# Values of two attention groups, and outputs and statistics of the second, laid out in DRAM with longer rows, and row halves and sums in a third ring buffer

## The chip, the cores and the metric

The kernel runs on one core of a Trainium2 chip. The metric is the time of one execution on the device in microseconds (us); smaller is better. The core has five engines that run their own instruction streams and wait for each other through semaphores: PE (matrix products), DVE (vectors), ACT (scalar functions and copies), POOL (general) and SP, which here issues nearly all transfers between DRAM and the on-chip memory, in one fixed order.

## The reference, cut to what matters

One decoder block over 1024 tokens of 1024 numbers, in float32:

```python
h = rms_norm(x, g_pre_mix)
z = h @ w_in                                  # q, k, v | conv input (2 x 1024) | two gates
# 3 groups of 8 heads of 64; group g attends with dilation 1, 4, 16 and windows 128, 512, 2048:
s = q @ k.T / 8 + bias;  lse = logsumexp(s);  o_g = exp(s - lse) @ v      # per group and head
o = sum_g softmax_g(lse)[g] * o_g             # the three groups merged per head
y_attn = o @ w_attn_out
y_conv = silu(layer_norm(depthwise_conv31(u * sigmoid(gate)))) @ w_conv_out + b
x = x + rms_norm((sigmoid(z_ga) * y_attn + sigmoid(z_gc) * y_conv) @ w_mix_out)
x = x + rms_norm(swiglu_ffn(rms_norm(x)))     # hidden width 2816
```

## The kernel before, in words

Every float32 operand of a matrix product is split into a high part (a cast on ACT) and a low part (a subtraction on DVE or POOL), and a product is three matmuls: high x high, high x low, low x high. The work runs in stages, by the time of the profile: start and first norm (0 to 44 us), gates and conv inputs by plain products (L305, L307, L309; to 109), pairs of weight tiles by a 2x2 Winograd scheme (L321 to L323; q, k and conv inputs, to 555), the value projections with the attention woven in (to about 870), conv and attention outputs and the mix (to about 1134), the FFN's input pairs by the same scheme (to 1510) and its output (L1843).

A Winograd pair takes two loads of 128x1024, `row1` and `row2`, and makes from their quarters the sums s12 and s34 (L215/L216 and L222/L223, on POOL in the q/k stretch, on DVE elsewhere). Each is split by `both` (ACT's cast L195, then the subtraction L196); L231/L232 split the last quarter. The products are copied out of PSUM by ACT (L335, L340, L345) before PE goes on. While pairs run, POOL also adds up channels (L706) and DVE works on the convolution (L684). In the gates, the normalised input is split on DVE at L584 after ACT's cast, and weights by ACT L188 and DVE L189; ACT L1179 and DVE L1180 split other operands.

`v()` makes the values of four heads at a time (L940, L942, L944) and interleaves them with attention steps (`beat`, `tick`). Its weights w_v are loaded and split some ticks after the call by `timed`; ACT copies the products into a tile x (L950, L952) and SP stores it to the DRAM tensor dv (L927). The attention takes 12 head pairs (three groups, four pairs) of eight steps: scores (L1038), bias and minimum on DVE (L1041, the bias tile comes by L477 from the DRAM tensor rep), exponential on ACT (L1051), transposes (L1074, copies L1079/L1080), product with the values (L1095/L1097, values loaded by L903 to L908 and split by L916/L917), reduction on DVE into the output tile O (L1102). For the first two groups O goes to the DRAM tensor datt and the statistics to dst (L1060, L1064); `merge` reads both back (L887, L893) in the order of the third group. dact holds the activated conv channels (L1237).

Tiles come from pools of equal buffers that are used in turn: `slot` (tag b, 43 buffers of 128x1024), `ring` (tag d, 2 buffers of the same size; O of groups 0 and 1 and, in the mix, the new x) and `half` (tag c, 11 of 128x512). A new tile waits until the last reader of the tile that held its buffer is done. The order of instructions on each engine is the order in which the code is written, with `later` and `timed` putting steps some ticks on. SP works its list in order; each transfer also waits for the one that was issued eight before it.

Of the kernel before, what the change touches and what calls it, by code (L numbers as in the profile page):

```python
# [43 lines left out]
PLAIN = 2  # L44

LAST = 5
NSLOT = 43

NRING = 2
NHALF = 11  # L50


# [10 lines left out]
class Build:  # L63
# [108 lines left out]
    def load_ahead(self, i):  # L172
        while self.sent < min(len(self.jobs), i + 1):
            j = self.sent
            src, n, _ = self.jobs[j]
            self.raw[j] = self.slot()
            self.nc.sync.dma_start(self.raw[j][:, :n], src)
            self.sent += 1

# [19 lines left out]
    def quarters(self, i, c):  # L199


        nc = self.nc
        if c == 0:
            self.hl[i] = {}
        o = self.hl[i]
        r1, r2 = self.raw[i - 1], self.raw[i]
        a11, a12, a21, a22 = r1[:, :H], r1[:, H:], r2[:, :H], r2[:, H:]
        add = self.wsplit.tensor_tensor
        l, r = slice(0, H), slice(H, 2 * H)
        if c == 0:  # L210
            h, w = self.both(r1)
            o["A11"], o["A12"] = (h[:, l], w[:, l]), (h[:, r], w[:, r])
        elif c == 1:
            self.s12 = self.slot()
            add(self.s12[:, l], a21, a22, op=OP.add)  # L215
            add(self.s12[:, r], self.s12[:, l], a11, op=OP.add)  # L216
        elif c == 2:
            h, w = self.both(self.s12)
            o["S1"], o["S2"] = (h[:, l], w[:, l]), (h[:, r], w[:, r])
        elif c == 3:  # L220
            self.s34 = self.slot()
            add(self.s34[:, l], a11, a21, op=OP.add)  # L222
            add(self.s34[:, r], self.s12[:, r], a12, op=OP.add)  # L223
            self.s12 = None
        elif c == 4:
            h, w = self.both(self.s34)
            o["S3"], o["S4"] = (h[:, l], w[:, l]), (h[:, r], w[:, r])
            self.s34 = None
        else:
            x = self.slot(F32R)  # L230
            nc.scalar.copy(x[:, l], a22)  # L231
            add(x[:, r], a22, f(x[:, l]), op=OP.subtract)  # L232
            o["A22"] = (x[:, l], x[:, r])
            del self.raw[i], self.raw[i - 1], self.hl[i]
# [662 lines left out]
    def values(self, g, hp):  # L897

        x = self.slot()
        d = x.rearrange("p (u e) -> p u e", u=8)  # L900
        src = self.d_v[g, hp]
        if g == 0:
            self.nc.sync.dma_start(d, src.rearrange("(u p) e -> p u e", p=128))  # L903
        elif g == 1:
            for b in range(2):
                self.nc.sync.dma_start(d[:, b::2, :], src.rearrange("(b p c) e -> b p c e", b=2, c=4)[b])
        else:
            self.nc.sync.dma_start(d, src.rearrange("(p u) e -> p u e", u=8))  # L908
        return x

    def value_parts(self, x, i):

# [7 lines left out]
    def v(self, g, hg, now, then):  # L920

        nc = self.nc
        W = self.timed(now, then, 6, 15)

        def out(i, x):
            for e in range(2):
                nc.sync.dma_start(self.d_v[g, 2 * hg + e].rearrange("(t p) c -> p t c", p=128)[:, i - 2:i + 2],  # L927
                                  x.rearrange("p (t e c) -> p t e c", t=4, e=2)[:, :, e])
            self.vn += i == 6

        for i in range(0, 8, 2):
            ps = self.bank()
            for e in range(2):
                t = slice((i + e) * 128, (i + e + 1) * 128)
                o = ps[:, e * 256:(e + 1) * 256]
                for kt in range(KT):
                    hi, lo = W[kt // 4]
                    s = slice((kt % 4) * 256, (kt % 4 + 1) * 256)
                    a, b = self.hH[kt][:, t], self.hL[kt][:, t]
                    nc.tensor.matmul(o, a, hi[:, s], start=kt == 0, stop=False)  # L940
                    self.beat()
                    nc.tensor.matmul(o, a, lo[:, s], start=False, stop=False)  # L942
                    self.beat()
                    nc.tensor.matmul(o, b, hi[:, s], start=False, stop=kt == KT - 1)  # L944
                    self.beat()
                    if kt % 2:
                        self.tick()
            if i % 4 == 0:
                x = self.slot()
                nc.scalar.copy(x[:, :H], ps)  # L950
            else:
                nc.scalar.copy(x[:, H:], ps)  # L952
                self.later(2, lambda i=i, x=x: out(i, x))
                x = None

# [67 lines left out]
    def att_s(self, a, p, V, u):  # L1023
# [16 lines left out]
        for hh in range(2):  # L1040
            nc.vector.tensor_tensor_reduce(sp[:, hh * 256:hh * 256 + n], ps[:, hh * 256:hh * 256 + n],  # L1041
                                           bt[:, hh * 256 + 256 - n:(hh + 1) * 256], 1.0, 3e38, OP.add, OP.min,
                                           st[:, g, u, hh:hh + 1])
        a.update(g=g, hp=hp, u=u, blocks=blocks, sp=sp, V=V, p=p, n=n)

    def att_e(self, a):
        nc = self.nc
        sp, n, g, u = a["sp"], a["n"], a["g"], a["u"]
        st = a["p"][4]
        for hh in range(2):  # L1050
            nc.scalar.activation(sp[:, hh * 256:hh * 256 + n], sp[:, hh * 256:hh * 256 + n], AF.Exp, scale=-1.0,  # L1051
                                 bias=st[:, g, u, hh:hh + 1], accum_out=st[:, g, u, 2 + hh:3 + hh])
        if u == 7 and g < 2:
            self.tokens_out(g, self.d_st[g, a["hp"]], st[:, g])

    def tokens_out(self, g, dst, src):

        if g == 0:
            d = dst.rearrange("(u p) e -> p u e", p=128)
            self.nc.sync.dma_start(d, src)  # L1060
        else:
            d = dst.rearrange("(b p c) e -> b p c e", b=2, c=4)
            for b in range(2):
                self.nc.sync.dma_start(d[b], src[:, b::2, :])  # L1064

    def att_t(self, a):

# [15 lines left out]
    def att_p(self, a):  # L1083
# [5 lines left out]
        for hh in range(2):  # L1089
            o = hh * 128  # L1090
            for i, kb in enumerate(a["blocks"]):
                c = (kb % 4) * 256 + hh * 128
                v = a["V"][kb // 4]
                s = slice((hh * nb + i) * 128, (hh * nb + i + 1) * 128)
# [4 lines left out]
            yield 0  # L1099
        if u == 0:  # L1100
            self.O = self.ring() if g < 2 else self.slot()
        nc.vector.tensor_reduce(self.O[:, u * 128:(u + 1) * 128].rearrange("p (h c) -> p h c", h=2),  # L1102
                                ps[:, :256].rearrange("p (h e c) -> p h c e", h=2, e=2), AX.X, OP.add)
        if u == 7:
            if g < 2:
# [226 lines left out]
def build(ctx, tc, aps):  # L1332
# [38 lines left out]
    B.d_q = {n: [B.dram.tile([128, H], F32, name=f"dq{n}_{p}") for p in range(FT // 2)]  # L1371
             for n in ("A11", "A12", "A22", "S1", "S2", "S3", "S4")}
    B.d_att = {(g, hp): B.dram.tile([T, 128], F32, name=f"datt{g}{hp}") for g in range(2) for hp in range(4)}
    B.d_v = {(g, hp): B.dram.tile([T, 128], F32, name=f"dv{g}{hp}") for g in range(3) for hp in range(4)}
    B.d_ot = [B.dram.tile([128, 1024], F32, name=f"dot{p}") for p in range(2)]
    B.d_st = {(g, hp): B.dram.tile([T, 4], F32, name=f"dst{g}{hp}") for g in range(2) for hp in range(4)}

# [581 lines left out]
```

## Time and profile before

| what | us |
| --- | --- |
| median of 3 runs | 1733.87 (1732.55 to 1734.95) |
| the profiled execution | 1728.74 |
| its span (first to last instruction) | 1726.9 |
| PE busy in the span | 1703.5 |
| DVE, ACT, POOL busy | 1237.1, 793.7, 462.5 |
| values and attention, 555 to 870: PE busy | 308.61 of 315.00 |

Times in the rows of the profile are from the start of the span. In a row of the timeline stand start, duration, engine, line, operation, out<-in with their shapes, and in brackets the idle time of the engine just before and what ended it. In a row of waits stand the waiting engine and line, what it waited for, the total in us, the number of waits and the longest. Names give the pool: b is a slot, d a ring, c a half, p PSUM. In a row on DMA issues stand the number of issues, the size of one and the median time from issue to landing.

### The profile page before, as it was taken

To read this page: it belongs to the slowest core of one execution; us is meant where nothing else is said; L and a number is where in the kernel's file an instruction comes from. 1 tells how busy PE (TensorE), PEld (TensorE's weight loads), DVE (VectorE), ACT (ScalarE), POOL (GpSimd) and SP (SyncE) were. 2 spreads that over 40 slices of the span, in tenths; PEclk is the share of its full clock that TensorE was granted. 3 is DMA by queue.
4 is the path that set the end of the run, shared out by engine and by line. 5 is a ranking of instruction groups with operands and counts; after the bars stand their busy time and mean duration, and the time that the engine had idled before them with its cause. 6 is when DMAs were issued, how large, how long until landed. Compare 5 with 4: busy or idle time off the path is not lost.

```text
span 1726.9 us, 24514 instructions
## 1 busy us (share of the span) xinstructions
PE 1703.5 (99%) x8698; PEld 1448.2 (84%) x8698; DVE 1237.1 (72%) x2217; ACT 793.7 (46%) x1552; POOL 462.5 (27%) x337
## 2 busy tenths in 40 slices
PE   8999999999999999999999999999999999999998
PEld 7778888887888999999788888888888888888886
DVE  6879988789998576687664855676556555677686
ACT  6344343434444486667622346643333333454453
POOL 0017777787786043443300120000000000000000
PEclk9999999999999999999999999999999999999999
DMA  4342344345667898988945732223322322395334
GB/s 164 125 160 86 110 160 133 135 159 184 206 164 194 246 257 200 245 227 213 310 145 187 275 107 93 83 73 112 126 92 92 112 108 92 137 363 159 107 126 153
DMA packets 185398, 277.03 MB, mean 160 GB/s; under 512 B 55185, under 2 KB 106892, under 8 KB 185276
## 3 DMA queue, kind: packets, MB, share of 16 engines
q1 hardware_dynamic: 184876, 274.97, 50.2%
q8 instruction: 68, 1.11, 0.3%
q14 instruction: 54, 0.44, 0.1%
q10 hardware_dynamic: 288, 0.27, 0.0%
q0 software_dynamic: 112, 0.24, 0.0%
HBM read 184.81 MB, written 95.33 MB: 162 GB/s over the span
## 4 chain that ended last, share of the span: by engine, by line
PE 86%; POOL 5%; DVE 3%; DMA 3%; ACT 2%; issue 2%; SPq 0%; DVEq 0%; POOLq 0%; ACTq 0%
PE p L321 13%; PE p L322 13%; PE p L323 13%; PE p L1843 12%; PE p L1572 5%; PE p L305 5%; PE p L307 5%; PE p L309 5%; PE p L942 2%; PE p L940 2%; PE p L944 2%; POOL b L196 2%; PE p L554 2%; PE p L1038 2%; PE p L1074 2%
## 5 line engine op out<-in xcount | busy, mean ns | idle before, releaser
L321 PE MATMUL p<-b,b 128*128 128x512 f32 x1204 | 469.4, 390 | 3.7 <-ACT c L335 2.4
L323 PE MATMUL p<-b,b 128*128 128x512 f32 x1204 | 468.8, 389 | 0.2 <-POOL b L196 0.2
L322 PE MATMUL p<-b,b 128*128 128x512 f32 x1204 | 468.5, 389 | 0.0
L321 PEld LDWEIGHTS p<-b,b 128*128 128x128 f32 x1204 | 226.0, 188 | 53.7 <-ACT c L335 3.2
L323 PEld LDWEIGHTS p<-b,b 128*128 128x128 f32 x1204 | 226.0, 188 | 48.5 <-POOL b L196 1.3
L322 PEld LDWEIGHTS p<-b,b 128*128 128x128 f32 x1204 | 226.0, 188 | 46.4
L195 ACT CAST b<-b 128x1024 fp32r<-128x1024 f32 x131 | 137.8, 1052 | 178.4 <-DVE b L216 50.9
L1843 PE MATMUL p<-b,b 128*128 128x512 f32 x924 | 209.6, 389 | 0.0
L1843 PEld LDWEIGHTS p<-b,b 128*128 128x128 f32 x924 | 173.4, 188 | 36.0
L196 POOL TENSOR_TENSOR b<-b,b 128x1024 fp32r<-128x1024 f32 x66 | 158.8, 2406 | 116.3 <-ACT b L195 108.1
L196 DVE TENSOR_TENSOR b<-b,b 128x1024 fp32r<-128x1024 f32 x65 | 79.5, 1222 | 128.9 <-ACT b L195 128.9
L684 DVE SCALAR_TENSOR_TENSOR p<-b,par,p 128x511 f32<-128x511 f32 (+14 forms) x232 | 163.4, 738 | 0.0
L305 PE MATMUL p<-b,b 128*128 128x512 f32 x368 | 147.6, 401 | 0.0
L309 PE MATMUL p<-b,b 128*128 128x512 f32 x368 | 146.2, 397 | 0.0
L307 PE MATMUL p<-b,b 128*128 128x512 f32 x368 | 146.1, 397 | 0.0
L940 PE MATMUL p<-b,b 128*128 128x256 f32 x384 | 115.3, 300 | 0.0
L942 PE MATMUL p<-b,b 128*128 128x256 f32 x384 | 114.6, 298 | 0.0
L944 PE MATMUL p<-b,b 128*128 128x256 f32 x384 | 114.5, 298 | 0.0
L1180 DVE TENSOR_TENSOR b<-c,b 128x512 fp32r<-128x512 f32 x101 | 69.9, 693 | 46.9 <-ACT b L1179 46.6
L1179 ACT CAST b<-c 128x512 fp32r<-128x512 f32 x101 | 62.4, 618 | 63.8 <-DMA c<-dqA 19.8
L1179 ACT CAST b<-b 128x512 fp32r<-128x512 f32 x117 | 72.4, 619 | 40.6 <-DVE b L387 13.7
L1180 DVE TENSOR_TENSOR b<-b,b 128x512 fp32r<-128x512 f32 x117 | 80.3, 690 | 14.8 <-ACT b L1179 13.1
(226 smaller groups left out, 2994.1 us busy)
## 6 DMA issues: line engine op xcount, KB each, us to landing
b<-w_in SPq DMA_DIRECT2D x53, 512.0 KB, 5.7
b<-w_fi SPq DMA_DIRECT2D x44, 512.0 KB, 4.9
dk<-c SPq DMA_DIRECT2D x48, 256.0 KB, 5.7
dq<-c SPq DMA_DIRECT2D x48, 256.0 KB, 4.3
b<-dq SPq DMA_DIRECT2D x48, 256.0 KB, 8.9
b<-dk SPq DMA_DIRECT2D x48, 256.0 KB, 7.3
dqS<-c SPq DMA_DIRECT2D x44, 256.0 KB, 2.1
b<-w_fo SPq DMA_DIRECT2D x44, 256.0 KB, 5.3
```

Of the source, the lines that this page charges most:

```text
L196: self.wsplit.tensor_tensor(lo, x, f(hi), op=OP.subtract)
L305: nc.tensor.matmul(ps, hi[:, s], a, start=kt == 0, stop=False)
L307: nc.tensor.matmul(ps, hi[:, s], b, start=False, stop=False)
L309: nc.tensor.matmul(ps, lo[:, s], a, start=False, stop=kt == nk - 1)
L321: nc.tensor.matmul(ps, hi[:, s], a, start=first and kt == 0, stop=False, skip_group_check=True)
L322: nc.tensor.matmul(ps, hi[:, s], b, start=False, stop=False, skip_group_check=True)
L323: nc.tensor.matmul(ps, lo[:, s], a, start=False, stop=kt == 3, skip_group_check=True)
L684: nc.vector.scalar_tensor_tensor(A[i][:, j:], src[i][:, :H - j], w[i], A[i][:, j:], op0=OP.mult, op1=OP.add)
L940: nc.tensor.matmul(o, a, hi[:, s], start=kt == 0, stop=False)
L942: nc.tensor.matmul(o, a, lo[:, s], start=False, stop=False)
L1180: nc.vector.tensor_tensor(s[:, 512:512 + n], src, f(s[:, :n]), op=OP.subtract)
L1843: nc.tensor.matmul(acc[t], x, y, start=first and e == 0, stop=last and e == 2, skip_group_check=True)
```

## The change

The slots go from 43 to 42 and the rings from 2 to 3. The row1 loads, s12 and the values' output tile x move from slots to rings. The DRAM tensor dv of group 0 becomes 128 x 1024 (partition by token block and channel), so that it is stored by 128x512 and loaded by 128x1024. For group 1, `place` puts the eight blocks of 128 positions in another order on chip, so that values are loaded, and outputs and statistics stored, by one transfer with 2 KB rows (64 B for the statistics), where two with 512 B (16 B) were. In `v()` the loads of the next w_v are released 4 ticks after the call instead of 6, and their splits 16 instead of 15.

```diff
-NSLOT = 43
-NRING = 2
+NSLOT = 42
+NRING = 3
...
     def load_ahead(self, i):
...
-            self.raw[j] = self.slot()
+            self.raw[j] = self.ring() if kind == "row1" else self.slot()
...
         elif c == 1:
-            self.s12 = self.slot()
+            self.s12 = self.ring()
...
     def values(self, g, hp):
         x = self.slot()
-        d = x.rearrange("p (u e) -> p u e", u=8)
         src = self.d_v[g, hp]
         if g == 0:
-            self.nc.sync.dma_start(d, src.rearrange("(u p) e -> p u e", p=128))
+            self.nc.sync.dma_start(x, src)
         elif g == 1:
-            for b in range(2):
-                self.nc.sync.dma_start(d[:, b::2, :], src.rearrange("(b p c) e -> b p c e", b=2, c=4)[b])
+            self.nc.sync.dma_start(x.rearrange("p (b f) -> p b f", b=2),
+                                   src.rearrange("(b p c) e -> p b (c e)", b=2, c=4))
...
+    def place(g, u):
+        return u % 2 * 4 + u // 2 if g == 1 else u
...
     def v(self, g, hg, now, then):
-        W = self.timed(now, then, 6, 15)
+        W = self.timed(now, then, 4, 16)
         def out(i, x):
             for e in range(2):
+                if g == 0:
+                    nc.sync.dma_start(self.d_v[g, 2 * hg + e][:, (i - 2) * 128:(i + 2) * 128], x[:, e * H:(e + 1) * H])
+                    continue
...
             if i % 4 == 0:
-                x = self.slot()
-                nc.scalar.copy(x[:, :H], ps)
+                x = self.ring()
+            if g == 0:
+                nc.scalar.copy(x.rearrange("p (e t c) -> p t e c", e=2, t=4)[:, i % 4:i % 4 + 2],
+                               ps.rearrange("p (t e c) -> p t e c", t=2, e=2))
             else:
-                nc.scalar.copy(x[:, H:], ps)
+                nc.scalar.copy(x[:, (i % 4) * 256:(i % 4) * 256 + H], ps)
...
     def tokens_out(self, g, dst, src):
...
-            d = dst.rearrange("(b p c) e -> b p c e", b=2, c=4)
-            for b in range(2):
-                self.nc.sync.dma_start(d[b], src[:, b::2, :])
+            self.nc.sync.dma_start(dst.rearrange("(b p c) e -> p b (c e)", b=2, c=4),
+                                   src.rearrange("p (b c) e -> p b (c e)", b=2))
...
# statistics st[:, g, u], value blocks kb and output columns u are taken at place(g, u)
...
-    B.d_v = {(g, hp): B.dram.tile([T, 128], F32, name=f"dv{g}{hp}") for g in range(3) for hp in range(4)}
+    B.d_v = {(g, hp): B.dram.tile([T, 128] if g else [128, T], F32, name=f"dv{g}{hp}") for g in range(3) for hp in range(4)}
```

On PE, DVE, ACT and POOL the order of instructions stays the same; what moves is SP's list and the waits. Line numbers behind the edits grow by up to 13 (L927 becomes L935 or L933, L1064 becomes L1074, L1180 becomes L1193, L1237 becomes L1250).

SP at the third call of `v()`, around 612 us, before (dact are stores of the conv's activations, dv of values, dq loads for the attention):

```order
L1237 DMA dact_83<-b_5358 128x1024
L1237 DMA dact_84<-b_5374 128x1024
L177 DMA b_5389<-w_v 128x1024
L177 DMA b_5391<-w_v 128x1024
L1237 DMA dact_85<-b_5394 128x1024
```

and with the change:

```order
L1250 DMA dact_83<-b_5358 128x1024
L177 DMA b_5373<-w_v 128x1024
L177 DMA b_5375<-w_v 128x1024
L1250 DMA dact_84<-b_5378 128x1024
L1250 DMA dact_85<-b_5394 128x1024
```

The two loads of w_v stand one store earlier.

SP at the end of a head pair of the second group, around 823 us, before (rep is the source of the bias tile, dst takes the statistics):

```order
L873 DMA b_8643<-dk_117 64x1024 x2
L1064 DMA datt_220<-d_8376 512x1x128 x2
L908 DMA b_8672<-dv_232 128x1024
L477 DMA c_8682<-rep_980 128x2x256
L866 DMA b_8821<-dq_120 64x1024
L867 DMA b_8822<-dq_120 64x1024
L1064 DMA dst_243<-stat_8146 512x1x4 x2
```

and with the change:

```order
L873 DMA b_8634<-dk_117 64x1024 x2
L1074 DMA datt_220<-d_8368 128x2x512
L907 DMA b_8662<-dv_232 128x1024
L477 DMA c_8672<-rep_980 128x2x256
L866 DMA b_8811<-dq_120 64x1024
L867 DMA b_8812<-dq_120 64x1024
L1074 DMA dst_243<-stat_8139 128x2x16
```

One transfer stands in the place of two, ahead of the value load and the bias tile.

DVE with what each instruction waits for, at the split of the normalised input (first three rows, around 65 us) and at the first pair's s12 (last three, around 111 us), before:

```order
L584 TENSOR_TENSOR b_729<-b_251,b_695 128x1024 [waits DVE_49]
L579 SCALAR_TENSOR_TENSOR b_253<-b_253,gains,b_570 128x1024
L584 TENSOR_TENSOR b_750<-b_252,b_717 128x1024 [waits PE_49,Activation_49]
...
L1180 TENSOR_TENSOR b_1049<-b_253,b_1049 128x512 [waits Activation_49]
L215 TENSOR_TENSOR b_1058<-b_939 128x512 [waits DMAHW2_49,PE_49]
L216 TENSOR_TENSOR b_1058<-b_1058,b_937 128x512 [waits DVE_49]
```

and with the change:

```order
L584 TENSOR_TENSOR b_729<-b_251,b_695 128x1024 [waits PE_49]
L579 SCALAR_TENSOR_TENSOR b_253<-b_253,gains,b_570 128x1024
L584 TENSOR_TENSOR b_750<-b_252,b_717 128x1024 [waits PE_49,Activation_49]
...
L1193 TENSOR_TENSOR b_1049<-b_253,b_1049 128x512 [waits Activation_49]
L215 TENSOR_TENSOR d_1058<-b_939 128x512 [waits DMAHW2_49]
L216 TENSOR_TENSOR d_1058<-d_1058,d_937 128x512 [waits DVE_49]
```

The first L584 waits for PE now, and s12 (L215, a ring d) waits for its load alone.

More of the change, by code (lines that the diff above doesn't have):

```diff
@@ L174, in load_ahead @@
             j = self.sent
-            src, n, _ = self.jobs[j]
-            self.raw[j] = self.slot()
+            src, n, kind = self.jobs[j]
+            self.raw[j] = self.ring() if kind == "row1" else self.slot()
             self.nc.sync.dma_start(self.raw[j][:, :n], src)
@@ L899, in values @@
         x = self.slot()
-        d = x.rearrange("p (u e) -> p u e", u=8)
         src = self.d_v[g, hp]
         if g == 0:
-            self.nc.sync.dma_start(d, src.rearrange("(u p) e -> p u e", p=128))
+            self.nc.sync.dma_start(x, src)
         elif g == 1:
-            for b in range(2):
-                self.nc.sync.dma_start(d[:, b::2, :], src.rearrange("(b p c) e -> b p c e", b=2, c=4)[b])
+            self.nc.sync.dma_start(x.rearrange("p (b f) -> p b f", b=2),
+                                   src.rearrange("(b p c) e -> p b (c e)", b=2, c=4))
         else:
-            self.nc.sync.dma_start(d, src.rearrange("(p u) e -> p u e", u=8))
+            self.nc.sync.dma_start(x, src.rearrange("(p u) e -> p (u e)", u=8))
         return x
+    @staticmethod
+    def place(g, u):
+        return u % 2 * 4 + u // 2 if g == 1 else u
     def value_parts(self, x, i):
@@ L948, in v @@
             if i % 4 == 0:
-                x = self.slot()
-                nc.scalar.copy(x[:, :H], ps)
-            else:
-                nc.scalar.copy(x[:, H:], ps)
+                x = self.ring()
+            if g == 0:
+                nc.scalar.copy(x.rearrange("p (e t c) -> p t e c", e=2, t=4)[:, i % 4:i % 4 + 2],
+                               ps.rearrange("p (t e c) -> p t e c", t=2, e=2))
+            else:
+                nc.scalar.copy(x[:, (i % 4) * 256:(i % 4) * 256 + H], ps)
+            if i % 4:
                 self.later(2, lambda i=i, x=x: out(i, x))
@@ L1042, in att_s @@
                                            bt[:, hh * 256 + 256 - n:(hh + 1) * 256], 1.0, 3e38, OP.add, OP.min,
-                                           st[:, g, u, hh:hh + 1])
+                                           st[:, g, self.place(g, u), hh:hh + 1])
         a.update(g=g, hp=hp, u=u, blocks=blocks, sp=sp, V=V, p=p, n=n)
@@ L1048, in att_e @@
         sp, n, g, u = a["sp"], a["n"], a["g"], a["u"]
-        st = a["p"][4]
+        st = a["p"][4][:, g, self.place(g, u)]
         for hh in range(2):
             nc.scalar.activation(sp[:, hh * 256:hh * 256 + n], sp[:, hh * 256:hh * 256 + n], AF.Exp, scale=-1.0,
-                                 bias=st[:, g, u, hh:hh + 1], accum_out=st[:, g, u, 2 + hh:3 + hh])
+                                 bias=st[:, hh:hh + 1], accum_out=st[:, 2 + hh:3 + hh])
         if u == 7 and g < 2:
-            self.tokens_out(g, self.d_st[g, a["hp"]], st[:, g])
+            self.tokens_out(g, self.d_st[g, a["hp"]], a["p"][4][:, g])
     def tokens_out(self, g, dst, src):
@@ L1091, in att_p @@
             for i, kb in enumerate(a["blocks"]):
+                kb = self.place(g, kb)
                 c = (kb % 4) * 256 + hh * 128
@@ L1101, in att_p @@
             self.O = self.ring() if g < 2 else self.slot()
-        nc.vector.tensor_reduce(self.O[:, u * 128:(u + 1) * 128].rearrange("p (h c) -> p h c", h=2),
+        w = self.place(g, u)
+        nc.vector.tensor_reduce(self.O[:, w * 128:(w + 1) * 128].rearrange("p (h c) -> p h c", h=2),
                                 ps[:, :256].rearrange("p (h e c) -> p h c e", h=2, e=2), AX.X, OP.add)
```

## The prediction

> **What bounds the kernel now.** I read the page first (span, busy time, slices), then the waits of PE, then for each wait the timeline and the chain of waits around it.
>
> ```profile
> span 1726.9 us, 24514 instructions
> PE 1703.5 (99%) x8698; PEld 1448.2 (84%) x8698; DVE 1237.1 (72%) x2217; ACT 793.7 (46%) x1552; POOL 462.5 (27%) x337
> ...
> PE p L554 <- ACT b L530: 6.0, 1, 6.0
> PE p L1097 <- DVE c L1080: 3.7, 5, 1.2
> PE p L321 <- ACT c L335: 2.4, 2, 2.0
> PE p L1038 <- DVE stat L1041: 1.3, 1, 1.3
> PE p L321 <- ACT c L340: 1.0, 3, 0.6
> PE p L1095 <- DVE d L1102: 0.5, 1, 0.5
> PE p L1095 <- DVE b L1102: 0.3, 1, 0.3
> PE p L1038 <- DMA b<-dk: 0.2, 1, 0.2
> PE p L323 <- POOL b L196: 0.2, 1, 0.2
> ...
> 555.00:870.00 315.00, 308.61 (x2514) 299.43 (x2514) 219.06 (x666) 205.54 (x598) 104.15 (x121) 1.00 0.88 239
> ```
>
> PE is busy 1703.5 of 1726.9 us and the change takes no matmul away. So what can be won is idle time of PE: these nine rows of waits (total us, times, longest us) add up to 15.6, of which 6.0 at L554 come before any edited line. Of the 9.6 that remain, 6.0 lie in the attention stage (the rows of L1097, L1038 and L1095; the window row's 315.00 − 308.61 = 6.4 agrees), where the clock is full (1.00) and the DMA engines are 0.88 busy, and 3.6 lie around the Winograd pairs. Every term below is one of these rows.
>
> **The change part by part.**
>
> *Rows of DRAM.* The first group's values are stored in 2 KB instead of 512 B rows and loaded in 4 KB rows; the second group's values are loaded, and its outputs stored, in 2 KB rows. Each is four tensors of 1024x128 numbers, 512 KB: 4 x 4 x 512 KB = 8.4 MB in longer rows, no byte fewer. Two windows of that stage, in which DMA is busy throughout, bound the price:
>
> ```profile
> DMA packets 1593, 3.11 MB, mean 311 GB/s; under 512 B 105, under 2 KB 942, under 8 KB 1592
> ...
> DMA packets 3002, 2.96 MB, mean 269 GB/s; under 512 B 1151, under 2 KB 2431, under 8 KB 3000
> ```
>
> The first window (612 to 622 us) carries mostly longer rows, the second (823 to 834) mostly short ones. 8.4 MB at 269 GB/s are 31.2 us, at 311 GB/s 27.0: 4.2 us of DMA time in 315. That is spread over the stage and reaches PE only where a load is the late thing, so I take 0 for the row length itself, with ends 0 and −4.2. The Trainium skill ("DMA: Bandwidth & Descriptors", Specifications) puts the smallest transfer at line rate at 512 B; by that rule only the 16 B statistics gain, and the sum would have 0 here too. The trace half agrees: the window with the short rows moved 269 GB/s, a little less.
>
> *Place of the value weights in SP's queue.* The loads of w_v are released two ticks earlier, so they stand ahead of a store of dact that waits for ACT:
>
> ```profile
> 611.25 1.59 SPq L1237 DMA_DIRECT2D dact<-b  x2
> 612.93 2.43 SPq L177 DMA_DIRECT2D b<-w_v  x2
> 620.03 0.62 ACT L188 CAST b<-b 128x512 fp32r<-128x512 f32 x1 [1.56 <-DMA b<-w_v]
> ```
>
> The load is issued at 612.93 and ends ACT's idle at 620.03; DVE's L189 follows, DVE's L1041 stands behind it, and PE's L1038 waits 1.3 for that. Ahead of the two stores' end the load can go about 1.59/2 = 0.8 us earlier, and 512 KB less lies before it: at 311 GB/s 1.7 us at most. So it lands 0.8 to 2.5 earlier: −0.8 to −1.3 (the whole stall). I take −1.3, since 0.8 already counts without any help from the data and most of the 1.7 is needed by nobody else. The stores that are pushed back feed loads long after. At one place further on, w_v is moved past loads of the attention instead, a bias tile among them. 1 MB at 311 GB/s is 3.4 us; a bias tile that came 3.56 us late (next fence) cost PE 1.2. So that is one end, +1.2; I add 0, since an earlier w_v is mostly through before the tile is issued.
>
> *One store for two.* The second group's output goes out as one DMA, and its statistics too. Behind them in SP's queue stand a value load and then the bias tile (rep):
>
> ```profile
> 823.45 2.16 SPq L1064 DMA_DIRECT2D datt<-d  x2
> 826.37 0.39 SPq L477 DMA_DIRECT2D c<-rep  x1
> 832.33 0.29 DVE L1041 CUSTOM_DVE_ANT_0 c<-p,c 128x128 f32<-128x128 f32 x1 [3.56 <-DMA c<-rep]
> ...
> 833.50 0.30 PE L1097 MATMUL p<-b,c 128*128 128x64 f32 x1 [1.20 <-DVE c L1080]
> 856.25 0.30 PE L1097 MATMUL p<-b,c 128*128 128x64 f32 x1 [1.21 <-DVE c L1080]
> ...
> DVE c L1041 <- DMA c<-rep: 4.9, 2, 3.6
> ```
>
> DVE stood 3.56 us for this tile and 4.9 − 3.6 = 1.3 for the next one (the other of the two); behind both, L1080 came late and PE's L1097 stood 1.2 each time, 2.4 in all. The pair of stores takes 2.16, so with one alone the tile is issued at least 2.16/2 = 1.1 earlier. That covers nearly all of PE's 1.2, if the tile's landing follows its issue. It need not, because each DMA in this queue also waits for the one eight issues before it, and at 0.88 busy the engines set the landing. Ends 0 and −2.4; I take the half, −1.2.
>
> *Weights' first rows and the sums s12 in the ring.* Slots are reused in turn, so s12 waited for whatever held its slot. At the first pair that was a weight in use by PE; the chain of waits runs through it, and then DVE and ACT are late for PE:
>
> ```profile
> 111.66 0.69 DVE L215 TENSOR_TENSOR b<-b 128x512 f32<-128x512 f32 x1 [3.06 <-PE p L307]
> 117.14 0.62 ACT L1179 CAST b<-b 128x512 fp32r<-128x512 f32 x1 [1.25 <-DVE b L196]
> 119.27 0.50 PE L321 MATMUL p<-b,b 128*128 128x512 f32 x1 [1.99 <-ACT c L335]
> ```
>
> In the ring L215 needs only its load (the order printed with the change shows the PE wait gone), so it starts up to 3.06 earlier and everything behind it on DVE with it. ACT's L1179 gains what it waited (1.25) and what its DVE source gains; PE's 1.99 is smaller than 3.06, so I take −2.0, with 0 as the other end (if the copies ahead of L335 are late for another reason).
>
> Later the same slot reuse made ACT's cast of s12 wait for POOL's channel sum (L706), on which it does not depend:
>
> ```profile
> 324.51 1.05 ACT L195 CAST b<-b 128x1024 fp32r<-128x1024 f32 x1 [4.90 <-POOL b L706]
> 325.64 2.40 POOL L196 TENSOR_TENSOR b<-b,b 128x1024 fp32r<-128x1024 f32 x1 [1.16 <-ACT b L195]
> ...
> ACT b L195 <- POOL b L706: 22.4, 5, 4.9
> 412.00 0.50 PE L321 MATMUL p<-b,b 128*128 128x512 f32 x1 [0.56 <-ACT c L340]
> ```
>
> Freed, the cast runs beside L706, and POOL's L196 follows L706 without the 1.16. In this stretch POOL is the late engine: PE's L321 waits for L340, which stands on ACT behind casts that wait for POOL, as the last row shows in the worst case; the waits of PE asked for 340 to 460 us alone give the whole 1.0 of that row and the 0.2 of L323 <- L196. Five such pairs save about 1.16 each; I take the 1.2 of PE's two rows, ends 0 and −1.6 (each stall also delays the start of the next matmul a little).
>
> The second L335 wait (2.4 − 2.0 = 0.4), at the FFN's first pair, sits behind the same kind of chain: −0.2, half of it. Ends 0 and −0.4.
>
> *One slot fewer.* The relief through the rings starts with the first pair; before that, in the gates, 42 slots do the work of 43, and the split of the normalised input waits for PE to give one up:
>
> ```profile
> 66.49 1.23 DVE L584 TENSOR_TENSOR b<-b,b 128x1024 fp32r<-128x1024 f32 x1 [0.90 <-PE p L309]
> 72.82 0.39 PE L307 MATMUL p<-b,b 128*128 128x512 f32 x1
> 74.14 0.69 DVE L189 TENSOR_TENSOR b<-b,b 128x512 fp32r<-128x512 f32 x1 [5.83 <-ACT b L188]
> 77.72 0.69 DVE L189 TENSOR_TENSOR b<-b,b 128x512 fp32r<-128x512 f32 x1 [0.56 <-ACT b L188]
> 81.25 0.39 PE L309 MATMUL p<-b,b 128*128 128x512 f32 x1
> ```
>
> In the order the first L584 gains a PE wait, and the second gets its slot from a later product, that of the L307 at 72.82. It then starts at 73.2 instead of 66.49, 6.7 us later, of which 5.83 are the idle that stood before L189: 0.9 remain, and up to 2.4 where ACT's copies between the two are pushed as well. The second L189 ends at 78.41, and PE first reads its half near 81.25: 2.8 us of margin. I take +0.2; ends 0 and +2.4.
>
> The values' outputs now share the three rings with the attention's. Taken in turn, the closest reuse is the copy below, which gets the ring that the store above it empties:
>
> ```profile
> 647.68 0.36 SPq L1060 DMA_DIRECT2D datt<-d  x1
> 662.41 0.58 ACT L950 COPY b<-p 128x512 f32<-128x512 f32 x1 [0.90 <-PE p L944]
> ...
> dv<-b SPq DMA_DIRECT2D x24, 256.0 KB, 6.3
> datt<-d SPq DMA_DIRECT2D x8, 256.0 KB, 8.5
> ```
>
> 14.7 us lie between issue and reuse, and such stores land 6.3 and 8.5 us after issue: 0. The eight ACT copies in another shape move the same elements: 0.
>
> **The sum.** −1.3 −1.2 −2.0 −1.2 −0.2 +0.2 = −5.7 us. The profiled execution took 1728.74 us; the median of the runs is 1733.87, 5 us more, and the sum is carried to it unchanged: 1728.2.
>
> **The rivals.**
> *Long rows help all of the attention stage.* The Trainium skill ("Perfetto Trace Analysis", DMA Optimizations) says that small DMAs, under 2 KB, carry significant overhead per transfer, and that merging them helps most where DMA is the bound. As a mechanism of this kernel: loads land earlier everywhere at 0.88 busy, and all of the stage's 6.4 us go instead of 2.5. Then the sum is −9.6, 1724.3 us. Against it: only 0.2 of PE's waits name a DMA directly, and 269 against 311 GB/s is a small step.
> *The late thing is only exchanged.* DVE is still late by its own bunching (L1102 0.5 + 0.3, and two of the five L1097), the bias tile lands when the engines let it, and POOL's chain stays the slowest of its stretch. Then w_v and s12's first wait are all: −1.3 − 2.0 = −3.3, less what slots cost (+0.2): 1730.8, no difference that the runs can tell (0.2%, 3.5 us, is about what they can).
> *A ring is not free (slower).* In the attention stage an ACT copy of values or DVE's first L1102 of a head pair would then stand until a store has landed, 6.3 or 8.5 us after its issue, and hold the casts and score rows behind it; PE has about 1 us there before it stops, as its L1097 rows show. It decides when a store is issued less than 8.5 us before the ring's next use; 12 values' tiles and 8 outputs take a ring. Two such waits cost 2 x (6.3 − 1) = 10.6, and −5.7 + 10.6 = +4.9: 1738.8 us. Against it: the 14.7 us above.
>
> **How the numbers follow.** Forecast 0.52, exchange 0.24, long rows 0.14, ring 0.06; 0.04 is left for the end +1.2 of w_v and +2.4 of the slot together with gains that fail, which is slower too. About 0.05 of the forecast's share lies within 0.2% of no change (3.5 us, which is about what the runs can tell): faster 0.47 + 0.14 = 0.61, same 0.05 + 0.24 = 0.29, slower 0.06 + 0.04 = 0.10. The range goes from the long rows, less the 0.4 and 0.2 by which POOL's and the second L335's ends lie lower and the 1.2 by which two runs of the kernel before differ (1722.5), to just past no change (1735): the ring and the lowest ends lie beyond it.
>
> **What would show it.** Right: no PE wait of 1.99 at 119 and DVE's L215 without its 3.06; ACT's casts of s12 no longer ended by L706, and L340's row at 0; w_v issued near 612 and L188 without idle; the bias tiles issued 1.1 us sooner after the output store, L1097's row near 1.3. Wrong: the same totals of PE's waits under other lines, a wait of PE between 66 and 84 us, or DVE or ACT ended by SP's stores for a ring.

## The result and the profile after

| | before | after |
| --- | --- | --- |
| median of the runs, us | 1733.21 (1730.96 to 1734.95) | 1720.17 (1719.84 to 1720.51) |
| profiled execution, us | 1728.74 | 1720.29 |
| ratio of the runs | | 0.9932, 95% interval 0.9917 to 0.9947 |

The kernel became 13.0 us faster. The forecast was 5.7, and the result lies below its range (1722.5 to 1735). Two things stand out: the profiled executions differ by 8.45 us only, and the runs of before spread over 4 us, those of after over 0.7.

The page, the waits of PE (total us, times, longest) and the stage of the values and the attention, after:

```profile
span 1718.5 us, 24444 instructions
PE 1700.9 (99%) x8698; PEld 1449.9 (84%) x8698; DVE 1235.5 (72%) x2217; ACT 794.2 (46%) x1552; POOL 461.4 (27%) x337
```

```profile
PE p L554 <- ACT b L530: 6.1, 1, 6.1
PE p L1109 <- DVE c L1091: 2.0, 4, 0.7
PE p L1050 <- DMA b<-dk: 1.6, 2, 1.1
PE p L1107 <- DVE b L1115: 0.3, 1, 0.3
PE p L321 <- ACT c L340: 0.3, 1, 0.3
PE p L1326 <- ACT b L1332: 0.2, 1, 0.2
```

```profile
555.00:870.00 315.00, 310.76 (x2526) 301.45 (x2524) 218.06 (x672) 206.74 (x605) 100.68 (x120) 1.00 0.82 235
```

The rows of L335 and of L323 <- L196 are gone, L340's fell from 1.0 to 0.3, L1038's (now L1050) wait for DVE is gone and one for loads of k has grown from 0.2 to 1.6, and L1097's (now L1109) fell from 3.7 to 2.0. DMA's share of the stage fell from 0.88 to 0.82. The places that the prediction named, in the timeline after:

```profile
66.59 1.22 DVE L584 TENSOR_TENSOR b<-b,b 128x1024 fp32r<-128x1024 f32 x1 [2.94 <-PE p L307]
73.72 1.22 DVE L584 TENSOR_TENSOR b<-b,b 128x1024 fp32r<-128x1024 f32 x1 [4.71 <-PE p L307]
109.28 0.69 DVE L215 TENSOR_TENSOR d<-b 128x512 f32<-128x512 f32 x1
...
606.82 1.99 SPq L177 DMA_DIRECT2D b<-w_v  x2
613.22 0.62 ACT L188 CAST b<-b 128x512 fp32r<-128x512 f32 x1 [0.70 <-DMA b<-w_v]
...
814.04 0.36 SPq L1074 DMA_DIRECT2D datt<-d  x1
814.97 0.83 SPq L477 DMA_DIRECT2D c<-rep  x1
823.47 0.29 DVE L1053 CUSTOM_DVE_ANT_0 c<-p,c 128x128 f32<-128x128 f32 x1 [0.30 <-PE p L1050]
```

Both L584 wait for PE as forecast (73.72; the forecast was 73.2), at no cost to PE. L215 starts with no wait. w_v is issued 6.4 us before its cast where it was 7.1. The bias tile (rep) is issued 0.93 us after the output store where it was 2.92, and it has landed when DVE wants it at 823.47.

### The profile page after: what moved, and what is told of

The parts are those of the page before. It is cut to its first block, busy times and chain, and to the rows that moved or that the text cites. A ratio compares the mean times of both kernels' runs of the same rounds, so it can differ in the third digit from the quotient of the medians.

```text
span 1718.5 us, 24444 instructions
## 1 busy us (share of the span) xinstructions
PE 1700.9 (99%) x8698; PEld 1449.9 (84%) x8698; DVE 1235.5 (72%) x2217; ACT 794.2 (46%) x1552; POOL 461.4 (27%) x337
## 4 chain that ended last, share of the span: by engine, by line
PE 95%; DMA 2%; ACT 1%; DVE 1%; POOL 1%; issue 0%; DVEq 0%; SPq 0%; ACTq 0%; POOLq 0%
PE p L321 16%; PE p L322 16%; PE p L323 15%; PE p L1856 12%; PE p L305 5%; PE p L309 5%; PE p L307 5%; PE p L1585 5%; PE p L950 2%; PE p L952 2%; PE p L948 2%; PE p L554 2%; PE p L1050 2%; PE p L1085 2%; PE p L1109 1%; PE p L1107 1%
## 5 line engine op out<-in xcount | busy, mean ns | idle before, releaser
L321 PE MATMUL p<-b,b 128*128 128x512 f32 x1204 | 469.1, 390 | 0.3 <-ACT c L340 0.3
L323 PE MATMUL p<-b,b 128*128 128x512 f32 x1204 | 469.0, 390 | 0.0
L322 PE MATMUL p<-b,b 128*128 128x512 f32 x1204 | 468.9, 389 | 0.0
L323 PEld LDWEIGHTS p<-b,b 128*128 128x128 f32 x1204 | 226.1, 188 | 46.7
L1856 PE MATMUL p<-b,b 128*128 128x512 f32 x924 | 209.6, 389 | 0.0
L305 PE MATMUL p<-b,b 128*128 128x512 f32 x368 | 147.7, 401 | 0.0
L309 PE MATMUL p<-b,b 128*128 128x512 f32 x368 | 146.4, 398 | 0.0
L307 PE MATMUL p<-b,b 128*128 128x512 f32 x368 | 146.2, 397 | 0.0
L195 ACT CAST b<-d 128x1024 fp32r<-128x1024 f32 x86 | 90.4, 1051 | 105.1 <-POOL d L216 55.0
L196 POOL TENSOR_TENSOR b<-d,b 128x1024 fp32r<-128x1024 f32 x44 | 106.8, 2428 | 79.9 <-ACT b L195 72.5
L196 DVE TENSOR_TENSOR b<-d,b 128x1024 fp32r<-128x1024 f32 x42 | 51.3, 1221 | 101.0 <-ACT b L195 101.0
L1193 DVE TENSOR_TENSOR b<-c,b 128x512 fp32r<-128x512 f32 x101 | 71.0, 704 | 38.2 <-ACT b L1192 38.0
L1193 DVE TENSOR_TENSOR b<-b,b 128x512 fp32r<-128x512 f32 x117 | 80.1, 690 | 20.7 <-ACT b L1192 18.8
L1585 PE MATMUL p<-b,b 128*128 128x512 f32 x384 | 89.4, 392 | 0.0
```

The costliest lines, as they stand in the source:

```text
L196: self.wsplit.tensor_tensor(lo, x, f(hi), op=OP.subtract)
L305: nc.tensor.matmul(ps, hi[:, s], a, start=kt == 0, stop=False)
L307: nc.tensor.matmul(ps, hi[:, s], b, start=False, stop=False)
L309: nc.tensor.matmul(ps, lo[:, s], a, start=False, stop=kt == nk - 1)
L321: nc.tensor.matmul(ps, hi[:, s], a, start=first and kt == 0, stop=False, skip_group_check=True)
L322: nc.tensor.matmul(ps, hi[:, s], b, start=False, stop=False, skip_group_check=True)
```

## The experiments

All times are against the kernel before on the same chip, whose median was 1733.5, 1732.3 and 1731.0 us in the three groups (e1 to e4, e5 to e8, e9 to e12). Where a run is compared with the changed kernel in us, the two medians come from different groups; by the ratios the same differences come out within 0.7 us.

### One part alone: rings, layouts, ticks; and the kernel before again

e1, the kernel before with (shortened):

```diff
-NSLOT = 43; NRING = 2
+NSLOT = 42; NRING = 3
-            self.raw[j] = self.slot()
+            self.raw[j] = self.ring() if kind == "row1" else self.slot()
-            self.s12 = self.slot()
+            self.s12 = self.ring()
```

> The kernel before with 42 slots, 3 rings, row1 and s12 in rings, and nothing else. Theory 1 (in the profiled executions PE came 2.3 us earlier at the first pair, 3.2 us at 350 to 530 us and 0.7 us at the FFN's first pair, all by s12's and row1's rings): its profiled execution is 6.2 us shorter than that of the kernel before (1728.74), PE waits of L321 gone, the attention stage as before (6.0 us of PE waits). Theory 2 (the runs of the kernel before are 4.5 us longer than its profiled execution because of transfers in the attention stage, which another execution lands later): the timed gain is the same 6.2 us, ratio 0.9964, and its runs still spread over 3 us or more. Rival (what varies lies in the pairs' stretch): timed gain 9 to 11 us, ratio 0.994 to 0.995, spread under 1 us.

e2, the kernel before with the diff of `values`, `place`, `tokens_out`, `out` and `d_v`, but `x = self.slot()`.

> The kernel before with the DRAM layouts of the change alone (longer rows, one transfer for two; the values' output tile in a slot). Theory 1: the bias tiles come earlier, PE's L1097 waits fall by 1.5 us, the wait at 119 us stays (2.0): profiled 1.5 us shorter. Theory 2 (transfers of the attention stage make the runs of the kernel before vary): timed gain 4 to 6.5 us, ratio 0.9963 to 0.9977, spread small. Rival (rows longer do nothing but save issues): timed gain 0 to 1.5 us, ratio 0.999 to 1.

e3, the kernel before with `timed(now, then, 4, 16)`.

> The kernel before with the value weights released at tick 4 and split at tick 16, and nothing else. Theory 1: L1038's wait of 1.3 us at 622 us is gone: 1 to 1.7 us shorter, ratio 0.999 to 0.9994. Rival (w_v only pushes the transfers behind it): 0, or up to 1.2 us longer.

e4, the kernel before unchanged.

> The kernel before once more, for a second profiled execution. Theory 2: if it is longer than 1728.74, the extra PE waits lie in the attention stage (555 to 870 us) under L1038, L1095 and L1097, and the waits at 119 and 350 to 460 us are the same to 0.1 us. Rival: the extra waits lie in the pairs' stretch.

| | median us | ratio, 95% interval |
| --- | --- | --- |
| e1 rings alone | 1736.29 | 1.0021 (1.0009 to 1.0033) |
| e2 layouts alone | 1729.30 | 0.9973 (0.9963 to 0.9984) |
| e3 ticks alone | 1731.77 | 0.9997 (0.9984 to 1.0011) |
| e4 before again | 1733.84 (one run) | |

These three parts alone add up to −0.09%; the whole change brings −0.68%. The whole has a fourth part, the values' tile in a ring, which has no run alone (e8 below is everything but that part). The interval of e3 holds 1, and PE in e3 still waits 1.62 us at 624: against theory 1, the earlier release alone does not remove that wait. e2 has the size that theory 2 gave, but its runs still spread over 7 us; its profiled execution is 0.6 us longer than the first one of before, against theory 1. Rings alone make it slower, against both theories, although PE's waits among the pairs are gone in e1's profile just as in that of the whole change. The waits of PE in e1, 109 to 555 us:

```profile
PE p L321 <- ACT c L340: 0.2, 1, 0.2
```

By the start of the same matmul in both, e1 is 5.3 us ahead of the profiled execution of before at 516 us and 9.1 behind at the end. What was won is lost in the attention stage. ACT of e1 there:

```profile
799.26 0.58 ACT L950 COPY b<-p 128x512 f32<-128x512 f32 x1 [4.15 <-DMA dot<-b]
...
827.01 0.62 ACT L916 CAST b<-b 128x512 fp32r<-128x512 f32 x1 [4.84 <-DMA dv<-b]
```

Two writes into a slot wait until a store that reads its last tile has landed. PE follows with waits of 1.81 and 3.72 us (and, arriving 5 us early at 619, it waits 3.79 behind the split of w_v), and then something that the first profile did not show at all. Columns: window, its length, busy us of PE, PEld, DVE, ACT, POOL (instructions), granted clock, DMA share, GB/s. Behind those two waits in e1:

```profile
801.36:811.36 10.00, 9.27 (x47) 8.78 (x47) 4.09 (x14) 3.86 (x16) 0.00 (x0) 0.66 0.40 119
828.76:838.76 10.00, 9.88 (x56) 8.74 (x57) 5.86 (x24) 5.93 (x22) 5.08 (x9) 0.83 0.88 242
```

The granted clock of PE is 0.66 and 0.83 over 10 us; in slices of 1 us it stands at 0.50 and then returns to 1.00. Missing clock is missing work: 10 x 0.34 = 3.4 and 10 x 0.17 = 1.7 us, on top of the waits. The kernel before does the same in its second profiled execution, e4. Three waits of PE:

```profile
120.28 0.50 PE L321 MATMUL p<-b,b 128*128 128x512 f32 x1 [1.99 <-ACT c L335]
625.02 0.38 PE L1038 MATMUL p<-b,b 128*128 128x256 f32 x1 [1.80 <-DVE stat L1041]
859.96 0.30 PE L1097 MATMUL p<-b,c 128*128 128x64 f32 x1 [1.99 <-DVE c L1080]
```

and the windows behind them, e4:

```profile
120.30:127.30 7.00, 7.00 (x24) 5.59 (x25) 4.91 (x7) 2.77 (x4) 0.00 (x0) 0.76 0.17 65
625.00:632.00 7.00, 6.98 (x46) 6.98 (x47) 4.76 (x19) 6.70 (x24) 0.61 (x1) 0.76 1.04 350
861.00:868.00 7.00, 7.00 (x37) 6.10 (x37) 6.33 (x25) 5.95 (x22) 2.72 (x2) 0.76 0.91 347
```

PE is busy throughout, but in the first window it issues 24 matmuls; the first profiled execution of before has 32 in a window of the same place:

```profile
120.30:127.30 7.00, 7.00 (x32) 5.78 (x31) 4.52 (x6) 3.79 (x6) 0.61 (x1) 1.00 0.03 12
```

The missing work is 3 x 7 x 0.24 = 5.0 us, and the two executions of one kernel differ by 1733.84 − 1728.74 = 5.1. The two numbers are not quite the same thing: by the start of the same matmul, e4 loses 1.0 us before 44 us, where the clock has no part in it, and 1.6, 1.3 and 1.1 us at the three places. Both theories of e4 are wrong: it is neither transfers alone nor waits in the pairs, since the waits are the same to within 0.8 us.

Two executions are few. But every run has its mean granted clock on record, and the 62 runs of before in the three groups give:

| mean granted clock | runs of before | their mean time, us |
| --- | --- | --- |
| 0.999 | 3 | 1728.0 |
| 0.998 | 8 | 1729.7 |
| 0.997 | 23 | 1731.8 |
| 0.996 | 18 | 1733.6 |
| 0.995 | 6 | 1735.3 |
| 0.994 | 4 | 1736.5 |

A thousandth of the clock is 1.7 us of work, and the times rise by 8.5 us over five thousandths, 1.7 each. The first profiled execution of before had 0.999, e4 0.996, and the four runs of the changed kernel had 0.999 to 1.000. So most of what makes the runs of before longer than its first profiled execution is clock, and in e4 the clock fell behind waits of PE of about 2 us.

### One part taken back

Each is the changed kernel with one part undone. e5: row1 and s12 in slots.

> The changed kernel with row1 and s12 in slots again (42 slots, 3 rings; the values' tile keeps its ring). Theory A (a wait of PE of about 2 us is paid twice: as idle time, and as some 4 us at half the granted clock after it): the 1.99 at 119 us is back with the halved clock behind it, the three waits of L340 and the second L335 too; 6.2 + 2 = 8.2 us longer than the changed kernel, ratio to the kernel before 0.998. Rival (the idle time is all): 6.2 us longer, ratio 0.9968. Theory B (the rings pay only because the values' weights come earlier): less than 4 us longer, ratio under 0.9955.

e6: the layouts as before.

> The changed kernel with the DRAM layouts of before (rings, the values' tile in a ring, tick 4). Theory A: the bias tiles come late behind two output stores, L1097's two waits of 1.2 us are back, one or two of them with 3 to 4 us at half clock: 2.5 to 6.5 us longer than the changed kernel, ratio 0.9947 to 0.997. Rival (row length is what frees the DMA engines for the whole stage): 8 us or more, DMA share of 555 to 870 us back at 0.88 from 0.82. Rival 2: under 1.5 us, ratio under 0.994.

e7: `timed(now, then, 6, 15)`.

> The changed kernel with w_v released at tick 6 and split at tick 15 again. Theory A: at 616 us PE, which comes 5 us earlier than in the kernel before, waits 3 to 4 us for w_v, as it did with the rings alone (3.8), and then runs some 6 us at half clock: 5 to 7 us longer than the changed kernel, ratio 0.996 to 0.9973. Rival (w_v is worth its 1.3 us): ratio under 0.9943.

e8: `x = self.slot()` in `v()`.

> The changed kernel with the values' output tile in a slot instead of a ring (42 slots, 3 rings, the rest as changed). Theory C (with the rings alone the attention stage lost time since ACT's copies at 799 and 827 us waited for slots that a store held until it landed; the values' tiles in slots are what makes slots short there): waits of 4 us of ACT for the landing of a store are back, each with a PE wait of 1.8 to 3.7 us and half clock behind it: 5 to 14 us longer than the changed kernel, ratio 0.996 to 1.002. Rival (those waits came from the late transfers of the old layouts): within 1 us of the changed kernel, ratio under 0.994.

| changed kernel with | median us | ratio, 95% interval |
| --- | --- | --- |
| nothing undone | 1720.17 | 0.9932 (0.9917 to 0.9947) |
| e5 row1, s12 in slots | 1767.70 | 1.0203 (1.0184 to 1.0221) |
| e6 old layouts | 1727.38 | 0.9973 (0.9961 to 0.9986) |
| e7 old ticks | 1720.43 | 0.9930 (0.9915 to 0.9945) |
| e8 values' tile in a slot | 1733.80 | 1.0008 (0.9996 to 1.0021) |

e7: the ticks are worth nothing that can be measured. PE waits 0.85 us at 616 in their absence, the clock stays full there, and by 844 e7 is 0.3 us behind: the changed kernel in its place waits 0.49 us for a load of k at 630, which e7 does not. Theory A is wrong; with the other parts in place the wait for the split is 0.85, not 3.8.

e8: 13.6 us, the whole gain, hang on the ring for the values' tile once there are 42 slots. ACT of e8 waits again where it did in e1:

```profile
634.76 0.59 ACT L963 COPY b<-p 128x512 f32<-128x512 f32 x1 [3.94 <-DMA dv<-b]
...
801.14 0.59 ACT L963 COPY b<-p 128x512 f32<-128x512 f32 x1 [4.37 <-DMA dot<-b]
```

PE follows with waits of 1.00 and 2.04 us, and the clock is halved behind both, at 638.6 and 805.8; the same matmuls come 2.8 and 5.5 us later across these two places. So theory C holds, though the first wait of PE is shorter than it gave: the third ring costs a slot, and the values' tile in that ring gives the slots back. It also explains the sum above: the three other parts together (e8) bring +0.08% where one by one they gave −0.09%, so what the sum lacks is the fourth part. e5 shows the same from the other side, far beyond every expectation: with 42 slots, and row1 and s12 in them, PE waits in nearly every pair of the first stretch. The waits of PE in e5:

```profile
PE p L321 <- ACT c L340: 21.1, 17, 1.7
PE p L554 <- ACT b L530: 6.0, 1, 6.0
PE p L321 <- ACT c L335: 5.1, 2, 3.2
PE p L323 <- POOL b L196: 4.2, 10, 0.4
```

It is 47.5 us longer than the changed kernel. It says what 42 slots cost without the rings, not what the rings bring to the kernel before; that is the 5.3 us of e1 up to 516 us.

e6: the layouts are worth 7.2 us, more than theory A gave. Its mechanism is there: the waits of L1097 add up to 6.7 us, the two longest are 2.27 and 2.02, and the clock is halved for 6.8 us from 830. DMA's share of the stage is 0.86, not 0.88.

### What in the layouts counts, and what a wait costs

e9: the changed kernel, group 0's values stored and loaded as before.

> The changed kernel with the first group's values stored and loaded in 512 B rows as before; the second group as changed. The layouts together are worth 7 us (0.9973 without them, 0.9932 with). Theory N (what counts is the number of transfers ahead of a bias tile in SP's queue, which only the second group's layout lowers): within 1.5 us of the changed kernel, ratio under 0.994. Theory R (long rows make the whole stage's transfers land sooner): 2 to 4 us longer, ratio 0.9943 to 0.9955.

e10: group 1's as before.

> The changed kernel with the second group's values, outputs and statistics as before (two transfers of 512 B or 16 B rows each); the first group as changed. Theory N: 5 to 7 us longer than the changed kernel, ratio 0.996 to 0.9973, waits of PE behind late bias tiles near 720, 830 and 855 us, the longest with half clock behind it. Theory R: 3 to 5 us, ratio 0.995 to 0.996.

e11: group 1's rows long, in two transfers (shown for the stores, shortened; the load of the values likewise):

```diff
-            self.nc.sync.dma_start(dst.rearrange("(b p c) e -> p b (c e)", b=2, c=4), src...)
+            for b in range(2):
+                self.nc.sync.dma_start(dst.rearrange("(b p c) e -> b p (c e)", b=2, c=4)[b], src...[b])
```

> The changed kernel with each of the second group's transfers split in two again, but with the long rows (2 KB, statistics 64 B). Theory N (number): like the one before, 5 to 7 us longer than the changed kernel. Theory R (row length): within 1.5 us of the changed kernel, ratio under 0.994.

e12, in `winograd` of the changed kernel:

```diff
+DOSE = {24: 3, 26: 4, 28: 5, 30: 6, 32: 7, 34: 8, 36: 9, 38: 10, 40: 12, 42: 14}
-        nc.scalar.copy(x1, X)
+        for _ in range(1 + DOSE.get(self.calls, 0)):
+            nc.scalar.copy(x1, X)
```

> The changed kernel with ACT's first copy of ten FFN pairs (every second) repeated 3, 4, 5, 6, 7, 8, 9, 10, 12 and 14 more times (the same copy again, no other result), so that PE waits there for 0 to some 5 us. Theory A (a wait of PE over some length lets the granted clock fall to half for about 4 us after it): waits up to about 1 us leave the clock at full, waits from about 2.5 us on always halve it, between the two it falls in some; each halving costs 1.7 to 3.5 us on top of the wait. Rival (the halved stretches have nothing to do with the waits): clock full throughout the FFN pairs, the time longer by the sum of the waits alone.

| | median us | ratio, 95% interval |
| --- | --- | --- |
| e9 group 0 old | 1720.58 | 0.9936 (0.9923 to 0.9948) |
| e10 group 1 old | 1725.89 | 0.9967 (0.9955 to 0.9979) |
| e11 group 1 long rows, two transfers | 1720.07 | 0.9935 (0.9922 to 0.9947) |
| e12 waits put in | 1763.51 (one run) | |

Group 0's rows bring nothing that the runs can tell, group 1's 5.7 us, and the number of transfers nothing: theory N is wrong (e11), and theory R holds for group 1 alone. In e10 the bias tile near 820 us comes late. From the chain of waits of e10:

```profile
811.61 8.68 DMA b<-dk
820.30 0.02 issue
820.31 10.99 DMA c<-rep
...
832.63 0.42 PE p L1111
```

Its issue waits for a load of k that was under way for 8.68 us, and it lands 10.99 us after issue; PE waits 3.19 us, and the clock is halved from 832 to 839. The transfers between 800 and 832 us, in e10:

```profile
DMA packets 7429, 7.00 MB, mean 219 GB/s; under 512 B 2436, under 2 KB 6061, under 8 KB 7426
```

and in e11, where the tile lands in time:

```profile
DMA packets 4102, 7.28 MB, mean 228 GB/s; under 512 B 963, under 2 KB 2243, under 8 KB 4099
```

More bytes in 0.55 of the packets. The Trainium skill ("Perfetto Trace Analysis", DMA Optimizations) says that transfers under 2 KB carry significant overhead each and that larger ones help most where DMA is the bound; e10 against e11 agrees, and e9, where the time did not change, does not show it. Which of group 1's rows count is open: values and outputs (512 B to 2 KB) and statistics (16 B to 64 B) change together in e10 and e11. The statistics are a rival to be taken seriously. Their stores of 8 KB, in e10 and in e11 (640 to 860 us; a landing is known for one of the eight in each, at 825 and 823 us):

```profile
dst<-stat SPq DMA_DIRECT2D x8, 8.0 KB, 10.0
...
dst<-stat SPq DMA_DIRECT2D x8, 8.0 KB, 1.4
```

The same bytes took 10.0 us to land in rows of 16 B and 1.4 in rows of 64 B. What each kind of row costs at the DMA engines was not measured apart.

e12 makes the price of a wait plain. Of the waits put in, those of 0.44, 1.05, 1.67 and 2.29 us left the clock full in this execution, those of 2.91 us and more halved it. Four of the nine:

```profile
1306.92 0.50 PE L322 MATMUL p<-b,b 128*128 128x512 f32 x1 [2.29 <-ACT c L339]
1348.22 0.50 PE L322 MATMUL p<-b,b 128*128 128x512 f32 x1 [2.91 <-ACT c L339]
1391.75 0.79 PE L322 MATMUL p<-b,b 128*128 128x512 f32 x1 [3.53 <-ACT c L339]
1529.48 0.79 PE L322 MATMUL p<-b,b 128*128 128x512 f32 x1 [6.61 <-ACT c L339]
```

and the 10 us behind each:

```profile
1306.92:1316.92 10.00, 10.00 (x44) 8.28 (x45) 5.03 (x7) 4.12 (x7) 0.00 (x0) 1.00 0.01 2
1348.22:1358.22 10.00, 10.00 (x37) 8.07 (x38) 3.46 (x4) 4.07 (x6) 0.00 (x0) 0.83 0.00 0
1391.75:1401.75 10.00, 10.00 (x32) 8.03 (x33) 2.44 (x4) 4.06 (x6) 0.00 (x0) 0.72 0.00 0
1529.48:1539.48 10.00, 10.00 (x35) 8.07 (x36) 4.72 (x7) 5.69 (x11) 0.00 (x0) 0.78 0.01 3
```

The wait of 2.91 us costs 10 x 0.17 = 1.7 us more, that of 3.53 us 2.8. The rival, that the time grows by the waits alone, is out: over the FFN this execution falls 41.1 us behind the profiled execution of the changed kernel, the nine waits add up to 28.0, and half of the time in which PE worked at half clock is 10.9.

But length alone does not decide: 1.99 us at the first pair left the clock full in the first profiled execution of before and halved it in e2, e3 and e4, and waits of 2.38 us (e8) and 2.02 us (e6) left it full. At half clock PE stays for 3.4 us (the row at 1348: 1.7 missing at half clock) or twice that.

The traces show more of what decides. In each trace the starts of the halved stretches lie whole multiples of 3.413 us apart (in e4 148 and 217 of them behind the first, in e5 74, 93, 112 and 308). So the clock can be read in steps of that length, and PE's idle time counted step by step. Three steps around the wait of 2.29 us in e12, and three around that of 2.91:

```profile
1301.86:1305.28 3.42, 2.77 (x13) 1.95 (x11) 0.00 (x0) 3.18 (x6) 0.00 (x0) 1.00 0.93 329
1305.28:1308.69 3.41, 1.77 (x8) 1.46 (x9) 0.85 (x1) 2.99 (x5) 0.00 (x0) 1.00 0.04 18
1308.69:1312.10 3.41, 3.41 (x17) 2.81 (x16) 1.58 (x3) 1.12 (x2) 0.00 (x0) 1.00 0.00 0
...
1342.82:1346.24 3.42, 2.49 (x12) 1.72 (x10) 0.00 (x0) 3.26 (x6) 0.00 (x0) 1.00 0.78 260
1346.24:1349.65 3.41, 1.43 (x6) 1.21 (x7) 0.50 (x1) 3.30 (x6) 0.00 (x0) 1.00 0.15 61
1349.65:1353.06 3.41, 3.41 (x9) 2.64 (x9) 1.92 (x3) 0.50 (x2) 0.00 (x0) 0.50 0.00 0
```

The first wait straddles two steps, with 0.65 and 1.64 us of idle time, and the clock stays full. The second leaves 3.41 − 1.43 = 1.98 us in one step, and the next step runs at half clock. Over all 14 traces, their first 10 us and the last of PE's work aside, each of the 13 steps with 1.98 us or more of idle time was followed by a halved step, none with 1.08 or less was, and of the 37 between 12 were. The wait of 2.38 us in e8 splits into 1.38 and 0.99, that of 2.02 in e6 into 0.86 and 1.17. What decides between 1.1 and 1.95 us stays open: at one place, near 718 us, 1.40 us halved the clock in e10 and 1.43 did not in e6, and at the first pair the first execution of before had 1.94 in one step.

The Trainium skill ("TensorE: Matmul & The Clock Gate", Part 1) has free-running windows of about 3.4 us, and half rate after one that was idle. The length of the slow stretches and their starts agree; that 1.1 to 2 us of idle time in a window can bring them does not agree with a whole idle window.

## Why the prediction was wrong

The place of each gain by the start of the same matmul, in us: the forecast, the two first profiled executions (1728.74 to 1720.29), and the execution e4 against after (1733.84 to 1720.29), which is nearer to a usual run:

```
place                          forecast   first profile   e4
start, before 44 us                 0          +0.4      −0.6
first pair, 119 us               −2.0          −2.3      −3.9
POOL's stretch, 350 to 520 us    −1.2          −3.2      −3.3
w_v, 621 to 640 us               −1.3          −1.0      −2.3
bias tiles, 820 to 865 us        −1.2          −1.5      −2.6
FFN's first pair                 −0.2          −0.7      −0.7
one slot fewer, 60 to 112 us     +0.2           0         0
sum                              −5.7          −8.3     −13.4
```

**"The sum is carried to it unchanged" failed, by 4.6 us** (13.0 less 8.45). The prediction saw that the median of before lay 5 us over the profiled execution and took that for a constant. Most of it was the halved clock behind three of the very waits that the sum removes (up to 1.7 us each, at 119, 625 and 861 us in e4). That the one execution profiled before the forecast missed all three was luck, and it hid the price. After the change the longest wait behind the start is 1.14 us, the clock stays full, and the runs spread over 0.7 us. The waits that the prediction counted were there; the price of a wait was put too low.

**POOL's stretch, mis-sized: −3.2 for −1.2.** The mechanism is as forecast (the casts of s12 no longer wait for L706; that row is gone from ACT's waits, and L340's fell to 0.3). The end given, −1.6, counted rows of waits. The starts of the matmuls show 0.3 to 0.9 at each of seven places (353, 393, 412, 452, 457, 510, 515 us); at four of them the wait before the matmul was 0.12 us or less, so rows of waits hold only a part of what such a place costs.

**First pair: right in place and in size** (−2.3 for −2.0, the clock aside). The FFN's pair came to −0.7, past its end of −0.4.

**w_v: wrong.** It is issued earlier and the wait at 621 is gone, as forecast. But e7 shows the same time without the earlier release, and in e3, with the release alone, the wait is still there (1.62 us). The stall went down the line, to a load of k. The prediction's other end, a bias tile that comes late behind w_v, came true without a price: DVE waits 3.38 us for one at 632.73, and PE does not wait behind it.

**"One store for two": wrong mechanism, and "I take 0 for the row length" failed.** The bias tiles near 820 and 845 us come in time, but e11 has two transfers and loses nothing; it is the row length of group 1 (e10, 5.7 us with the clock). Mean GB/s over two windows was too blunt a price: in e10 what counted near 820 us was one load of 8.68 us in front of one tile. The rival of the long rows was right for group 1 and wrong for group 0; nor did all of the stage's 6.4 us of idle time go, as it has it: 315.00 − 310.76 = 4.2 remain.

**One slot fewer and the ring: right where it looked, but the swap was not weighed.** No PE wait came between 60 and 112 us, and neither ACT nor DVE waited for a store to leave a ring. The prediction held the values' tile in a ring to be worth 0; e8 puts it at 13.6 us, since without it 42 slots do not carry the attention stage.

## What to carry to other kernels

Price a wait of the matrix engine of more than about 1 us at its length and, in many executions, 1.7 to 3.4 us of halved clock behind it; when the median of the runs is longer than the profiled execution, look at the clock of both before taking the difference for a constant. Take a change of buffers as one piece: what gives a slot and what takes it do not have prices of their own, as the rings alone (slower by 0.21%), everything but the values' tile (no gain) and all together (0.68% faster) show. Where transfers are the bound, ask which load stands ahead of the tile that the engines wait for; long rows there were worth 5.7 us, the same edit elsewhere nothing.

## What the runs showed of the hardware

The granted clock of PE fell to 0.50 behind single waits of 1.36 us (e12, at 849) to 6.6 us (e12), and behind every wait of 2.9 us or more, or already within it, after the first 10 us. In each trace the falls come on a grid of 3.413 us, and what counts is PE's idle time within one step of it: 1.98 us or more always (13 of 13), 1.08 or less never, between them 12 of 37. The clock stayed at half for one step or two; the second step was halved where the wait reached 0.4 us or more into the first (six times), and once, in e1 at 802 us, without that. No run shows what decides between 1.1 and 1.95 us.

A store of 8 KB landed 10.0 us after its issue in rows of 16 B (e10) and 1.4 us in rows of 64 B (e11), one store each.
